# A streaming encoder layer on one core: the Vector engine's dependent instructions recorded apart

## The chip, the cores and the metric

The kernel runs on one core of a Trainium2 chip. The metric is the device time of one launch in microseconds (us); lower is better. Five engines work side by side, each with its own in-order queue: PE (matrix products; PEld is its weight load), DVE (vector work), ACT (activations and copies), POOL and SP (which here issues the transfers). They wait for one another, and an engine waits for its own earlier results, through semaphores.

## The reference

One layer of a hybrid trunk over 2048 prompt rows and 32 sample rows of width 1024. After a LayerNorm, one projection yields the inputs of two branches. Branch A is attention over a band of nine 64-row chunks. Branch B is a gated delta rule over 64-row chunks; cut to what matters here:

```python
m = einsum(k_beta, kb) * decay * strict
t_inv = triangular_solve(eye + m, eye)        # 64 x 64 for each chunk and head
u = t_inv @ v_beta
w = t_inv @ (k_beta * exp(gc))
def step(s, ...):                             # chunk after chunk
    v_new = u_c - w_c @ s
    o_c = (q_c * exp(gc_c)) @ s + qk_c @ v_new
    s = s * exp(g_last) + k_dec.T @ v_new
```

Both branches are gated, projected, merged and projected again, added to the scaled input, and normalised.

## The kernel before

The rows are done in two halves of 1024. For each half, phase B (the delta rule) is followed by phase A (attention); the merge of the branches and the last projection follow at the end. All the while 48 column tiles of the input weight, and a narrow 49th, are fetched, scaled, split into two 16-bit parts (`divide`, line 613) and multiplied with the normalised rows (`multiply`, line 657). These products write the tile `pj`. They are the filler of the PE queue throughout both phases.

**Phase B** works on blocks of eight chunks for a pair of heads, eight blocks a half, plus one block for the sample rows at the end of the second half: 17 blocks. For each block `system` (line 1160) makes the 64x64 systems, `solve` (line 1211) inverts their 32x32 diagonal parts with all 128 partitions at once by forward substitution, and `inverse` puts the 64x64 inverses together. Two `solve` streams run, so two blocks may be in substitution at once. `substitute` (line 1229) has 31 steps; each is a product `sys_t <- sys_u, sys_p` and a subtraction `sys_u <- sys_u, sys_t`, both on DVE, the second needing the first and the next product needing the second. That is 17 x 31 = 527 pairs.

`chain` (line 1305) then goes through the chunks in order. One step of it is a relay between PE and DVE: PE makes `x <- state, k_bd`, DVE makes `r`, PE makes `x <- r, u_bd`, DVE makes `vn`, PE makes `x <- vn, kd_bd`, DVE makes the new `state`. There are 132 steps. `tail` (line 1337) normalises a block's output; the lengths of its rows are worked out in the small tile `ms`.

**What sets the order.** Nothing here is scheduled by hand. Every piece of work is a Python generator, a stream, with a clock of its own. `Flow.run` (line 171) takes the stream with the lowest clock off a heap and lets it record instructions until its next `yield`. `Flow.spend` (line 191) charges each recorded instruction a modelled price and a hop (`HOP_SAME`, 0.12, where the stream's last instruction was on the same engine, `HOP` or `HOP_PE` otherwise) and moves the stream's clock. Instructions that stand between two yields therefore come out as neighbours, and each engine runs its instructions in exactly the recorded order. Where an instruction needs the result of an earlier one of its own engine, it carries a wait for it.

**Other names.** For each of the 49 weights `divide` computes a norm, a power of two `w_scale`, and from it the factors `w_inv` and `w_half`, which undo the scaling when the products leave PE. `h_scale` holds the same for the rows, made once by `norm_params`. In `system`, `inv`, `sc` and `gcb` (read there as `e_p`) lead from the squared lengths of k to the factors of the system's elements. `lengths` and `by_token` use the PSUM tile `b`, as do transposes.

Of the kernel before, what the change touches and what calls it, by code (L numbers as in the profile page):

```python
# [16 lines left out]
ALU = mybir.AluOpType  # L17
# [35 lines left out]
HOP_PE, HOP, HOP_SAME = 0.1, 0.2, 0.12  # L53
# [101 lines left out]
class Flow:  # L155
# [5 lines left out]
        self.heap, self.n, self.busy = [], 0, {}  # L161
        self.cur = Stream(None, 0.0)

    def push(self, s):
        self.n += 1
        heapq.heappush(self.heap, (s.clock, self.n, s))

    def start(self, gen, at=None):
        self.push(Stream(gen, self.cur.clock if at is None else at))
# [1 line left out]
    def run(self, until=None):  # L171
        outer = self.cur
        while self.heap and (until is None or until.at is None):
            s = heapq.heappop(self.heap)[2]
            self.cur = s
            try:
                what = next(s.gen)
            except StopIteration:
                continue
            if what is None:  # L180
                self.push(s)
            elif isinstance(what, float):
                s.clock = max(s.clock, what)
                self.push(s)
            else:
                what.ask(s)
        outer.clock = max(outer.clock, self.cur.clock)
        self.cur = outer
        assert until is None or until.at is not None, "a stream waits for good"
# [78 lines left out]
def trunk(ctx: ExitStack, tc: tile.TileContext, x_p, x_s, cache_k, cache_v, st_conv, st_gdn,  # L268
# [4 lines left out]
    flow = Flow()  # L273
# [98 lines left out]
    def norm_params(sp):  # L372

        prm0 = sp.tile([2 * KD, P], F32, name="prm0")
        dma(prm0[0:KD], ln0_g.rearrange("(k p) -> k p", p=P))
        yield dma(prm0[KD:2 * KD], ln0_b.rearrange("(k p) -> k p", p=P))
        yield bank["b"]
        ps = pt("b")
        PE.transpose(ps[:, 0:2 * KD], prm0[:], ident[0:2 * KD, 0:2 * KD])
        yield  # L380
        V.tensor_copy(ln0gT[:], ps[:, 0:KD])
        V.tensor_copy(ln0bT[:], ps[:, KD:2 * KD])
        bank["b"].give()

        top = sp.tile([P, 2, KD], F32, name="top")
        V.scalar_tensor_tensor(out=top[:, 0], in0=ln0gT[:], scalar=-1.0, in1=ln0gT[:], op0=ALU.mult, op1=ALU.max)
        V.scalar_tensor_tensor(out=top[:, 1], in0=ln0bT[:], scalar=-1.0, in1=ln0bT[:], op0=ALU.mult, op1=ALU.max)
        V.scalar_tensor_tensor(out=top[:, 0], in0=top[:, 0], scalar=D ** 0.5, in1=top[:, 1], op0=ALU.mult, op1=ALU.add)
        V.tensor_tensor(out=top[:, 1], in0=top[:, 0], in1=top[:, 0], op=ALU.mult)
        V.tensor_reduce(out=h_scale[:, 0:1], in_=top[:, 1], axis=AX.X, op=ALU.add)  # L390
        yield
        yield from power(h_scale[:, 1:2], h_scale[:, 0:1])
        V.reciprocal(out=h_scale[:, 2:3], in_=h_scale[:, 1:2])
        V.tensor_scalar(out=ln0gT[:], in0=ln0gT[:], scalar1=h_scale[:, 1:2], scalar2=None, op0=ALU.mult)
        V.tensor_scalar(out=ln0bT[:], in0=ln0bT[:], scalar1=h_scale[:, 1:2], scalar2=None, op0=ALU.mult)
        scaled.done()
# [186 lines left out]
    def fetch(jobs):  # L583
# [26 lines left out]
            yield raw_gate  # L610
        front_w.done()

    def divide():

        while True:
            job, raw, t = yield from q_raw.get()
            yield w_gate
            hi = wpool.tile([P, KD, P], F16, tag="whi", bufs=2, name="whi")
            lo = wpool.tile([P, KD, P], F16, tag="wlo", bufs=2, name="wlo")
            sc = w_scale[:, job.wid:job.wid + 1]  # L620
            yield t
            if job.half == 0:
                S.activation(out=hi[:], in_=raw[:], func=AF.Square, accum_out=w_sq[:])
                yield
                yield from power(sc, w_sq[:])
                inv = w_inv[:, job.wid:job.wid + 1]
                V.reciprocal(out=inv, in_=sc)
                V.tensor_scalar(out=inv, in0=inv, scalar1=h_scale[:, 2:3], scalar2=None, op0=ALU.mult)
                V.tensor_scalar(out=w_half[:, job.wid:job.wid + 1], in0=inv, scalar1=0.5, scalar2=None, op0=ALU.mult)
            src, main = raw[:, :, 0:job.cols], hi[:, :, 0:job.cols]  # L630
            S.activation(out=src, in_=src, func=AF.Copy, scale=sc)
            for i in range(2):
                ks = slice(4 * i, 4 * i + 4)
                S.copy(out=main[:, ks], in_=src[:, ks])
                yield

                rest_ = lo[:, ks] if job.cols == P else hi[:, ks, job.cols:P]
                G.tensor_tensor(out=rest_, in0=src[:, ks], in1=main[:, ks], op=ALU.subtract)
                if i:
                    raw_gate.give()  # L640
                    q_w.put((job, hi, lo))
                yield
# [133 lines left out]
    def phase_b(half):  # L776
# [383 lines left out]
        def system(k):  # L1160

            nch = k.nch
            n = nch * CH
            k.par = yield from par_slots.take()
            yield k.qk_ready
            yield k.prep
            k.pn = yield from p_slots.take()
            kb, qkb = k.kb, k.qkb = k_bd[k.par], qk_bd[k.par]
            p_c = k.p_c = p_cs[k.pn]
            qk, e_in, sc = k.qk, k.e_in, k.sc  # L1170
            s_p = sc[:, 1, 0:nch]
            for h in range(2):
                (S.copy if h else V.tensor_copy)(out=bdv(kb, h, nch), in_=chunked(hv(qk, h)[:, 1, 0:n]))
            ss = bp.tile([P, 2, 8], F32, tag="ss", bufs=9, name="ss")
            k.rr = bp.tile([P, 8], F32, tag="rr", bufs=9, name="rr")
            yield bank["b"]
            ps = pt("b")
            yield from lengths(k, 1, ss, ps, p_c)
            bank["b"].give()
            inv = bp.tile([P, 8], F32, tag="inv", bufs=2, name="inv")  # L1180
            V.reciprocal(out=inv[:, 0:nch], in_=ss[:, 1, 0:nch])
            V.scalar_tensor_tensor(out=s_p, in0=inv[:, 0:nch], scalar=0.25, in1=k.beta, op0=ALU.mult, op1=ALU.mult)
            e_p = k.gcb[:].rearrange("p (c i) -> p c i", i=HD)
            V.tensor_tensor(out=e_p[:, 0:nch], in0=e_in[:, 0:nch], in1=bcast(s_p, nch), op=ALU.mult)
            yield

            for g0 in range(0, nch, 4):
                g1 = min(nch, g0 + 4)
                yield bank["b"]
                ps = pt("b")  # L1190
                for c in range(g0, g1):
                    PE.matmul(ps[:, (c - g0) * P:(c - g0 + 1) * P], kb[:, c, :], qk[:, :, c * CH:(c + 1) * CH],
                              start=True, stop=True)
                    yield
                pv = ps[:, 0:(g1 - g0) * P].rearrange("p (c a d) -> p c a d", a=2, d=HD)
                V.tensor_tensor(out=p_c[:, g0:g1], in0=pv[:, :, 1, :], in1=e_p[:, g0:g1], op=ALU.mult)
                yield
                for h in range(2):
                    V.tensor_tensor(out=qkb[HS[h], g0:g1, HS[h]], in0=hv(pv, h)[:, :, 0, :],
                                    in1=hv(e_in, h)[:, g0:g1], op=ALU.mult)  # L1200
                bank["b"].give()
                yield

            dv = pd[k.n % (2 * NP)][:].rearrange("(c k) (j i) -> k j c i", k=4, i=32)
            for q in range(4):
                b = q % 2
                t = dma(dv[q][:, 0:nch], p_c[q * 32:q * 32 + 32, 0:nch, b * 32:b * 32 + 32])
            q_sys.put((k, t))
            flow.start(side(k, ss))
# [19 lines left out]
        def substitute(sys_p, sys_u, sys_t):  # L1229
            for j in range(31):  # L1230
                nr = j // 4 + 1
                w = 31 - j
                if nr == 1:
                    V.tensor_scalar(out=sys_t[:, 0, 0:w], in0=sys_p[:, j, j + 1:32], scalar1=sys_u[:, 0, j:j + 1],
                                    scalar2=None, op0=ALU.mult)
                else:
                    V.tensor_tensor(out=sys_t[:, 0:nr, 0:w], in0=sys_u[:, 0:nr, j:j + 1].to_broadcast([P, nr, w]),
                                    in1=sys_p[:, j:j + 1, j + 1:32].to_broadcast([P, nr, w]), op=ALU.mult)
                V.tensor_tensor(out=sys_u[:, 0:nr, j + 1:32], in0=sys_u[:, 0:nr, j + 1:32],
                                in1=sys_t[:, 0:nr, 0:w], op=ALU.subtract)  # L1240
                yield
# [95 lines left out]
        def tail(k):  # L1337
# [14 lines left out]
            m1 = ms[:, 1, 0:nch]  # L1352
            yield
            V.tensor_tensor(out=m0, in0=m0, in1=m1, op=ALU.mult)
            V.tensor_tensor(out=m0, in0=m0, in1=m1, op=ALU.mult)
            V.tensor_scalar(out=m0, in0=m0, scalar1=1.0 / HD, scalar2=NORM_EPS, op0=ALU.mult, op1=ALU.add)
            yield
            rsqrt(m2, m0)
# [936 lines left out]
```

## Time and profile before

| | |
|---|---|
| median of 3 runs | 2122.08 us (2121.66 to 2124.06) |
| the profiled execution | 2124.96 us |
| its span, first to last instruction | 2123.1 us |
| PE busy | 1994.4 us, 94% |
| DVE busy | 1534.2 us, 72% |
| ACT busy | 978.7 us, 46% |
| POOL busy | 634.3 us, 30% |
| mean granted PE clock | 0.98 |

The profile is of one execution. Nearly every instruction is recorded by the helper at line 259, so groups are told apart by the tiles that they write and read (written `out<-in`). In the trace the substitutions run from 142 to 479 us (first half) and from 955 to 1324 us (second half); the steps of the chain run from 210 to 522 us and from 1017 to 1342 us. Matmuls are pipelined and the ends that the profile gives them are modelled, so "PE busy" is not PE at its peak.

### The profile page before, as it was taken

The page shows a single profiled execution, that of the slowest core. Times are in us where ns is not written, and L with a number is a line of the kernel's source. Part 1 is how long each engine was busy: PE and PEld are TensorE (multiplying, and loading weights), DVE is VectorE, ACT ScalarE, POOL GpSimd, SP SyncE. Part 2 cuts the span into 40 slices and gives each one's busy share as a digit, 9 for nine tenths or more (in the row PEclk, how much of TensorE's full clock was granted, in tenths as well). Part 3 has the DMA queues.
Part 4 walks back from the last instruction along what each step waited for, and adds up shares of the span by engine and source line. Part 5 has one row for each costly group of instructions (what it writes and reads, how often), then busy time and mean ns, then how long its engine had stood idle before and what let it go on. Part 6 is the DMA issues. An engine that isn't in the chain of part 4 may idle for free. (4 is left out here: it accounts for less than half of the span.)

```text
span 2123.1 us, 41363 instructions
## 1 busy us (share of the span) xinstructions
PE 1994.4 (94%) x15098; PEld 1422.5 (67%) x15098; DVE 1534.2 (72%) x4660; ACT 978.7 (46%) x2098; POOL 634.3 (30%) x708
## 2 busy tenths in 40 slices
PE   4999898999999999999899999999999988999998
PEld 4454665666465656666666676767776777988896
DVE  7689989884277768779898987347657667766676
ACT  5655544443465667564444443346656652111110
POOL 6243333232322122333233232310110223443343
PEclk9999999899999999999999999999999999999999
DMA  3223232222423233222223233332322435443331
GB/s 120 75 84 102 76 88 78 67 79 82 122 67 120 82 93 99 70 73 76 58 70 94 62 86 85 99 100 72 92 77 67 138 120 191 128 123 103 116 107 61
DMA packets 197719, 196.49 MB, mean 93 GB/s; under 512 B 79622, under 2 KB 147570, under 8 KB 197516
## 3 DMA queue, kind: packets, MB, share of 16 engines
q1 hardware_dynamic: 197516, 193.85, 30.9%
q8 instruction: 119, 1.95, 0.4%
q14 instruction: 84, 0.69, 0.1%
HBM read 135.91 MB, written 50.53 MB: 88 GB/s over the span
## 5 line engine op out<-in xcount | busy, mean ns | idle before, releaser
L259 PE MATMUL pj<-hi,whi 128*128 128x512 f16 (+2 forms) x1992 | 650.7, 342 | 8.6 <-POOL whi L259 3.0
L259 PE MATMUL pj<-hi,wlo 128*128 128x512 f16 (+2 forms) x1952 | 640.8, 341 | 0.4 <-POOL wlo L259 0.4
L259 PEld LDWEIGHTS <-whi 128*128 128x128 f16 x3984 | 416.0, 106 | 217.5 <-issue 11.2
L259 PE MATMUL pj<-lo,whi 128*128 128x512 f16 (+2 forms) x1992 | 461.9, 340 | 0.0
L259 POOL TENSOR_TENSOR wlo<-wraw,whi 128x512 f16<-128x512 f32 x192 | 228.6, 1193 | 630.1 <-ACT whi L259 345.1
L259 PEld LDWEIGHTS <-wlo 128*128 128x128 f16 x1952 | 205.5, 105 | 108.5 <-issue 8.9
L259 ACT CAST mh<-sg 128x256 fp32r<-128x256 f32 x64 | 25.9, 407 | 276.1 <-DVE sg L259 276.0
L259 DVE TENSOR_TENSOR sys_u<-sys_u,sys_t 128x60 f32<-128x60 f32 (+24 forms) x527 | 135.7, 258 | 18.2
L259 PE MATMUL a<-ghi,whi 128*128 128x256 f32 (+1 forms) x512 | 134.8, 293 | 7.1 <-DVE sg L259 6.8
L259 ACT ACTIVATE wraw<-wraw,w_scale 128x1024 f32<-128x1024 f32 (+1 forms) x98 | 111.4, 1137 | 59.2 <-DVE w_scale L259 57.1
L259 ACT CAST ph<-b 128x512 f16<-128x512 f32 (+2 forms) x224 | 92.6, 422 | 92.7 <-PE b L259 86.1
L259 PE MATMUL a<-ghi,wlo 128*128 128x256 f32 (+1 forms) x512 | 131.9, 287 | 0.0
L259 ACT CAST whi<-wraw 128x512 f16<-128x512 f32 (+1 forms) x196 | 119.4, 611 | 27.1 <-PE pj L259 24.2
L259 DVE TENSOR_TENSOR pl<-b,ph 128x512 f16<-128x512 f32 (+2 forms) x224 | 107.6, 484 | 28.9 <-ACT ph L259 28.0
L259 DVE TENSOR_TENSOR sys_t<-sys_u,sys_p 128x54 f32<-128x54 f32 (+21 forms) x459 | 123.6, 269 | 4.0
L259 ACT ACTIVATE sb<-sb,mx,unit 128x640 f32<-128x640 f32 (+4 forms) x128 | 109.0, 852 | 25.5 <-DVE mx L259 25.1
L259 DVE SCALAR_TENSOR_TENSOR acc<-raw,cwT,acc 128x512 f32<-128x512 f32 x144 | 113.2, 786 | 8.4 <-ACT acc L259 7.4
L259 POOL TENSOR_TENSOR w_scale<-w_scale,mhalf 128x1 f32<-128x1 f32 x49 | 31.0, 633 | 288.0 <-DVE w_scale L259 230.1
L259 PEld LDWEIGHTS a<-ghi,whi 128*128 128x128 f32 x512 | 99.3, 194 | 8.8 <-DVE sg L259 7.9
L259 PE MATMUL b<-ident,sb 128*128 128x128 f32 x560 | 98.8, 276 | 2.9 <-ACT tmp L259 0.6
L259 ACT COPY v_t<-o 128x64 f32<-128x64 f32 x132 | 27.5, 209 | 158.3 <-PE o L259 121.5
L259 PEld LDWEIGHTS a<-ghi,wlo 128*128 128x128 f32 x512 | 98.9, 193 | 0.4 <-DVE wlo L259 0.2
(350 smaller groups left out, 4238.9 us busy)
## 6 DMA issues: line engine op xcount, KB each, us to landing
wraw<-in_w_in SPq DMA_DIRECT2D x192, 256.0 KB
sg<-sig SPq DMA_DIRECT2D x112, 128.0 KB
sig<-sig SPq DMA_DIRECT2D x44, 256.0 KB
sys_p<-sol_p SPq DMA_DIRECT2D x17, 512.0 KB
x<-in_x_p SPq DMA_DIRECT2D x16, 512.0 KB
xt<-in_x_p SPq DMA_DIRECT2D x16, 512.0 KB
out_y_p<-xt SPq DMA_DIRECT2D x16, 512.0 KB
glo<-g SPq DMA_DIRECT2D x14, 512.0 KB
```

What stands on the lines that cost most here:

```text
L259: r = f(*a, **k)
```

## The change

No computation is added but one small product (half of `h_scale`'s third column, made once). Some yields are added and one group of instructions is moved:

- in `substitute` a yield stands between product and subtraction;
- in `system` and `tail` yields stand between the dependent small instructions on `inv`, `sc`, `gcb` and on `ms`;
- the factors `w_inv` and `w_half` are made by a stream of their own, `factors`, so that the scaling of the weight on ACT no longer follows them in one stream. Both come straight from the reciprocal, with two ready factors, where before the second was made from the first;
- a stream whose last instruction was on DVE is put back on the heap `HOP_SAME` later (`push(s, later)`): streams are taken up by when DVE would be ready for them, not by when their last instruction ends.

```diff
@@ -161,9 +161,9 @@
         self.heap, self.n, self.busy = [], 0, {}
         self.cur = Stream(None, 0.0)
 
-    def push(self, s):
+    def push(self, s, later=0.0):
         self.n += 1
-        heapq.heappush(self.heap, (s.clock, self.n, s))
+        heapq.heappush(self.heap, (s.clock + later, self.n, s))
 
     def start(self, gen, at=None):
         self.push(Stream(gen, self.cur.clock if at is None else at))
@@ -178,7 +178,8 @@
             except StopIteration:
                 continue
             if what is None:
-                self.push(s)
+
+                self.push(s, HOP_SAME if s.last == "V" else 0.0)
             elif isinstance(what, float):
                 s.clock = max(s.clock, what)
                 self.push(s)
@@ -391,6 +392,7 @@
         yield
         yield from power(h_scale[:, 1:2], h_scale[:, 0:1])
         V.reciprocal(out=h_scale[:, 2:3], in_=h_scale[:, 1:2])
+        V.tensor_scalar(out=h_scale[:, 3:4], in0=h_scale[:, 2:3], scalar1=0.5, scalar2=None, op0=ALU.mult)
         V.tensor_scalar(out=ln0gT[:], in0=ln0gT[:], scalar1=h_scale[:, 1:2], scalar2=None, op0=ALU.mult)
         V.tensor_scalar(out=ln0bT[:], in0=ln0bT[:], scalar1=h_scale[:, 1:2], scalar2=None, op0=ALU.mult)
         scaled.done()
@@ -610,6 +612,14 @@
             yield raw_gate
         front_w.done()
 
+    def factors(wid):
+
+        inv, half_ = w_inv[:, wid:wid + 1], w_half[:, wid:wid + 1]
+        V.reciprocal(out=half_, in_=w_scale[:, wid:wid + 1])
+        yield
+        V.tensor_scalar(out=inv, in0=half_, scalar1=h_scale[:, 2:3], scalar2=None, op0=ALU.mult)
+        V.tensor_scalar(out=half_, in0=half_, scalar1=h_scale[:, 3:4], scalar2=None, op0=ALU.mult)
+
     def divide():
 
         while True:
@@ -623,10 +633,7 @@
                 S.activation(out=hi[:], in_=raw[:], func=AF.Square, accum_out=w_sq[:])
                 yield
                 yield from power(sc, w_sq[:])
-                inv = w_inv[:, job.wid:job.wid + 1]
-                V.reciprocal(out=inv, in_=sc)
-                V.tensor_scalar(out=inv, in0=inv, scalar1=h_scale[:, 2:3], scalar2=None, op0=ALU.mult)
-                V.tensor_scalar(out=w_half[:, job.wid:job.wid + 1], in0=inv, scalar1=0.5, scalar2=None, op0=ALU.mult)
+                flow.start(factors(job.wid))
             src, main = raw[:, :, 0:job.cols], hi[:, :, 0:job.cols]
             S.activation(out=src, in_=src, func=AF.Copy, scale=sc)
             for i in range(2):
@@ -1178,8 +1185,11 @@
             yield from lengths(k, 1, ss, ps, p_c)
             bank["b"].give()
             inv = bp.tile([P, 8], F32, tag="inv", bufs=2, name="inv")
+            yield
             V.reciprocal(out=inv[:, 0:nch], in_=ss[:, 1, 0:nch])
+            yield
             V.scalar_tensor_tensor(out=s_p, in0=inv[:, 0:nch], scalar=0.25, in1=k.beta, op0=ALU.mult, op1=ALU.mult)
+            yield
             e_p = k.gcb[:].rearrange("p (c i) -> p c i", i=HD)
             V.tensor_tensor(out=e_p[:, 0:nch], in0=e_in[:, 0:nch], in1=bcast(s_p, nch), op=ALU.mult)
             yield
@@ -1236,6 +1246,7 @@
                 else:
                     V.tensor_tensor(out=sys_t[:, 0:nr, 0:w], in0=sys_u[:, 0:nr, j:j + 1].to_broadcast([P, nr, w]),
                                     in1=sys_p[:, j:j + 1, j + 1:32].to_broadcast([P, nr, w]), op=ALU.mult)
+                yield
                 V.tensor_tensor(out=sys_u[:, 0:nr, j + 1:32], in0=sys_u[:, 0:nr, j + 1:32],
                                 in1=sys_t[:, 0:nr, 0:w], op=ALU.subtract)
                 yield
@@ -1352,7 +1363,9 @@
             m1 = ms[:, 1, 0:nch]
             yield
             V.tensor_tensor(out=m0, in0=m0, in1=m1, op=ALU.mult)
+            yield
             V.tensor_tensor(out=m0, in0=m0, in1=m1, op=ALU.mult)
+            yield
             V.tensor_scalar(out=m0, in0=m0, scalar1=1.0 / HD, scalar2=NORM_EPS, op0=ALU.mult, op1=ALU.add)
             yield
             rsqrt(m2, m0)
```

The list of instructions on PE, ACT, POOL and SP is the same as before in kind and number; DVE has 4663 for 4662. The order differs on every engine from the first transposes of the rows on; on DVE and POOL nearly to the end, while PE's last 2296 matmuls and weight loads and SP's last 192 transfers stand as before. Numbers behind names tell buffers apart.

**DVE, first half, where one substitution ends and the next begins** (`sys_t_3594` and `sys_t_4173` before, `sys_t_3595` and `sys_t_4187` in the change). Before:

```order
L259 TENSOR_TENSOR sys_t_3594<-sys_u_3593,sys_p_3592 128x8x2
L259 TENSOR_TENSOR sys_u_3593<-sys_u_3593,sys_t_3594 128x8x2
L259 SCALAR_TENSOR_TENSOR zb_4315<-zb_4315,pj_4239 128x512
L259 TENSOR_SCALAR vn_4345<-x_659,sc_2854 128x64
L259 TENSOR_TENSOR kd_bd0_623<-b_4321,swap_4304 64x4x64 x2
L259 TENSOR_SCALAR sys_t_4173<-sys_p_4171,sys_u_4172 128x30
L259 TENSOR_TENSOR sys_u_4172<-sys_u_4172,sys_t_4173 128x30
L259 TENSOR_TENSOR sys_t_3594<-sys_u_3593,sys_p_3592 128x8
L259 TENSOR_TENSOR sys_u_3593<-sys_u_3593,sys_t_3594 128x8
```

In the change:

```order
L260 TENSOR_SCALAR sys_t_4187<-sys_p_4185,sys_u_4186 128x31
L260 SCALAR_TENSOR_TENSOR r_4386<-x_634,negc_633,v_t1_630 128x64
L260 TENSOR_TENSOR sys_t_3595<-sys_u_3594,sys_p_3593 128x8x2
L260 TENSOR_TENSOR sys_u_4186<-sys_u_4186,sys_t_4187 128x31
L260 TENSOR_TENSOR sys_u_3594<-sys_u_3594,sys_t_3595 128x8x2
L260 TENSOR_SCALAR sys_t_4187<-sys_p_4185,sys_u_4186 128x30
L260 TENSOR_SCALAR vn_4397<-x_634,sc_2824 128x64
L260 TENSOR_TENSOR sys_t_3595<-sys_u_3594,sys_p_3593 128x8
L260 TENSOR_TENSOR sys_u_4186<-sys_u_4186,sys_t_4187 128x30
L260 TENSOR_TENSOR e_in_4410<-gcb_4317,col_632 128x512
L260 SCALAR_TENSOR_TENSOR state_118<-state_118,sc_2824,x_634 128x64
L260 TENSOR_TENSOR sys_u_3594<-sys_u_3594,sys_t_3595 128x8
```

Before, each subtraction stands directly behind its product. In the change there is a step of the other substitution, of the chain or of another block between the two. In the whole order the subtraction is its product's direct neighbour 527 times before and 151 times in the change; the next product is the subtraction's direct neighbour 78 and 147 times. All pairs of direct neighbours of which the second needs the first and waits for it fall from 1071 to 574.

**DVE, the factors of one weight**, a little later. Before:

```order
L259 TENSOR_SCALAR w_scale_128<-w_scale_128 128x1
L259 RECIPROCAL w_inv_129<-w_scale_128 128x1
L259 TENSOR_SCALAR w_inv_129<-w_inv_129,h_scale_126 128x1
L259 TENSOR_SCALAR w_half_130<-w_inv_129 128x1
L259 SCALAR_TENSOR_TENSOR state_118<-state_118,sc_2854,x_659 128x64
L259 TENSOR_TENSOR kd_bd0_623<-b_4321,sc_3870 64x4x64
L259 TENSOR_SCALAR sys_t_4173<-sys_p_4171,sys_u_4172 128x29
```

In the change:

```order
L260 TENSOR_TENSOR sys_t_4187<-sys_u_4186,sys_p_4185 128x2x25
L260 TENSOR_SCALAR w_scale_128<-w_scale_128 128x1
L260 TENSOR_TENSOR sys_u_4186<-sys_u_4186,sys_t_4187 128x2x25
L260 RECIPROCAL w_half_130<-w_scale_128 128x1
L260 TENSOR_SCALAR vn_4487<-x_634,sc_2824 128x64
L260 TENSOR_TENSOR sys_t_4187<-sys_u_4186,sys_p_4185 128x2x24
L260 COPY sc_4469<-ex_4471 128x8
L260 TENSOR_SCALAR w_inv_129<-w_half_130,h_scale_126 128x1
L260 TENSOR_SCALAR w_half_130<-w_half_130,h_scale_126 128x1
L260 SCALAR_TENSOR_TENSOR state_118<-state_118,sc_2824,x_634 128x64
```

The three instructions on the factors, a run in which each needed the one before, now stand apart, with steps of the chain and of the substitution between them.

**PE, one step of the chain in the same stretch**, from the product with `r` to the product with `vn`; `pj` are the projections that fill the queue. Before:

```order
L259 MATMUL x_659<-r_4393,u_bd1_631 128x64
L259 LDWEIGHTS whi_4080
L259 MATMUL pj_4411<-hi01_152,whi_4080 128x512
L259 MATMUL o_661<-state_118,q_bd1_619 128x64
L259 LDWEIGHTS wlo_4081
L259 MATMUL pj_4411<-hi01_152,wlo_4081 128x512
L259 LDWEIGHTS whi_4080
L259 MATMUL pj_4411<-hi01_152,whi_4080 128x512
L259 LDWEIGHTS wlo_4081
L259 MATMUL pj_4411<-hi01_152,wlo_4081 128x512
L259 MATMUL x_659<-vn_4416,kd_bd1_625 128x64
```

In the change:

```order
L260 MATMUL x_634<-r_4386,u_bd1_606 128x64
L260 LDWEIGHTS whi_3948
L260 MATMUL pj_4323<-lo01_153,whi_3948 128x512
L260 MATMUL o_636<-state_118,q_bd1_594 128x64
L260 MATMUL b_4403<-ident_106,v_t0_629 128x128 x4
L260 LDWEIGHTS whi_3948
L260 MATMUL pj_4323<-lo01_153,whi_3948 128x512
L260 MATMUL x_634<-vn_4397,kd_bd1_600 128x64
```

Four projections stood between the two; now two and a row of transposes do. Over all 132 steps the mean number of projections ahead of the product with `vn`, counted from the last product into `x`, falls from 4.04 to 3.45, and ahead of the product with `r` from 4.80 to 4.52.

## The prediction

> **What bounds the kernel now.** I read the page's first part first, then the busy time by stretches, then who waited for whom.
>
> ```profile
> span 2123.1 us, 41363 instructions
> PE 1994.4 (94%) x15098; PEld 1422.5 (67%) x15098; DVE 1534.2 (72%) x4660; ACT 978.7 (46%) x2098; POOL 634.3 (30%) x708
> core 0: us, PE busy (x) PEld busy (x) DVE busy (x) ACT busy (x) POOL busy (x), PEclk, DMA share, GB/s
> 142.00:210.00 68.00, 62.84 (x392) 34.07 (x391) 63.90 (x205) 37.19 (x66) 25.58 (x37) 0.97 0.33 90
> 210.00:479.00 269.00, 248.06 (x1851) 168.58 (x1849) 236.42 (x853) 122.96 (x260) 87.41 (x108) 0.96 0.29 80
> ...
> 955.00:1017.00 62.00, 56.25 (x442) 39.31 (x441) 58.62 (x184) 29.97 (x59) 20.42 (x34) 0.94 0.25 70
> 1017.00:1324.00 307.00, 281.60 (x2416) 208.84 (x2415) 263.66 (x950) 130.96 (x303) 91.72 (x122) 0.98 0.30 77
> ...
> 1790.00:2123.00 333.00, 322.85 (x2012) 290.94 (x2012) 228.36 (x366) 39.59 (x112) 127.97 (x100) 0.98 0.35 109
> ```
>
> Over the whole span PE is the bound: 94% busy, and its list of work does not change. So the time can change only by the time in which PE stands still. The two substitution regions (the four middle rows, 706 us together) are where it stands: it is idle there for 706 - 648.8 = 57 us by these rows, and DVE is busy for 622.6 us, 88%. The last row, 333 us, holds the merge, whose PE order the change leaves alone.
>
> Who ends PE's waits, and DVE's, while the chain runs (142 to 1342 us)?
>
> ```profile
> PE x L259 <- DVE vn L259: 15.4, 22, 1.3
> PE x L259 <- DVE r L259: 11.9, 19, 1.3
> PE x L259 <- DVE state L259: 8.1, 11, 2.3
> ...
> PE x L259 <- DVE sys_t L259: 5.1, 2, 2.7
> DVE state L259 <- PE x L259: 31.2, 54, 2.6
> ...
> DVE r L259 <- PE x L259: 22.3, 29, 5.5
> DVE vn L259 <- PE x L259: 14.6, 29, 1.1
> ```
>
> PE waits 15.4 + 11.9 + 8.1 + 5.1 = 40.5 us for DVE in the chain (the last of these is put down to a neighbour of the chain's instructions). DVE waits 31.2 + 22.3 + 14.6 = 68.1 us for PE. Neither bounds the chain alone. One step as the timeline shows it:
>
> ```profile
> 304.71 0.33 PE L259 MATMUL x<-state,k_bd 128*128 128x64 f32 x2
> ...
> 305.29 0.20 DVE L259 TENSOR_TENSOR sys_u<-sys_u,sys_t 128x42 f32<-128x42 f32 x1
> 305.41 0.14 DVE L259 TENSOR_SCALAR w_scale<-w_scale 128x1 int32<-128x1 int32 x1
> 305.59 0.16 DVE L259 RECIPROCAL w_inv<-w_scale 128x1 f32<-128x1 f32 x1
> ...
> 305.79 0.21 DVE L259 TENSOR_SCALAR w_inv<-w_inv,h_scale 128x1 f32<-128x1 f32 x1
> ...
> 306.04 0.15 DVE L259 TENSOR_SCALAR w_half<-w_inv 128x1 f32<-128x1 f32 x1
> ...
> 306.20 0.86 DVE L259 TENSOR_TENSOR kd_bd<-b,swap 64x256 f32<-64x256 f32 x2
> ...
> 307.07 0.20 DVE L259 TENSOR_TENSOR sys_t<-sys_u,sys_p 128x35 f32<-128x35 f32 x1
> 307.31 0.20 DVE L259 TENSOR_TENSOR sys_u<-sys_u,sys_t 128x35 f32<-128x35 f32 x1
> ...
> 307.54 0.28 DVE L259 SCALAR_TENSOR_TENSOR r<-x,negc,v_t 128x64 f32<-128x64 f32 x1
> ...
> 307.88 0.43 PE L259 MATMUL x<-r,u_bd 128*128 128x64 f32 x2 [0.67 <-DVE r L259]
> ```
>
> PE had finished `x` at 305.04; `r` started at 307.54. For 2.5 us it stood in DVE's queue behind weight factors and substitution, and PE then lost 0.67 us. This queue is what the change shortens.
>
> **What a dependent neighbour costs.** Each row's first number is its start.
>
> ```profile
> 316.25 0.21 DVE L259 TENSOR_TENSOR sys_t<-sys_u,sys_p 128x52 f32<-128x52 f32 x1
> 316.50 0.21 DVE L259 TENSOR_TENSOR sys_u<-sys_u,sys_t 128x52 f32<-128x52 f32 x1
> 316.63 0.28 DVE L259 SCALAR_TENSOR_TENSOR r<-x,negc,v_t 128x64 f32<-128x64 f32 x1
> 316.83 0.41 DVE L259 COPY k_bd<-qk 64x512 f32<-64x512 f32 x1
> L259 DVE TENSOR_TENSOR sys_u<-sys_u,sys_t 128x60 f32<-128x60 f32 (+24 forms) x527 | 135.7, 258 | 18.2
> L259 DVE TENSOR_TENSOR sys_t<-sys_u,sys_p 128x54 f32<-128x54 f32 (+21 forms) x459 | 123.6, 269 | 4.0
> ```
>
> The subtraction needs the product before it and starts 0.25 us after it. `r` does not need the subtraction and starts 0.13 us after it, before its recorded end. A dependent neighbour therefore costs 0.12 us of the queue more than an independent one, most of it inside the recorded duration and not seen as idle time (the 18.2 us of idle over 527 subtractions are only the rest).
>
> The Trainium skill ("VectorE: DVE Perf Modes", section "The DRAIN you can't avoid") says otherwise: the next Vector instruction does not start until the pipe is empty, and a semaphore between two costs nothing extra. The trace disagrees, since `r` started 0.08 us before the subtraction's recorded end; by that rule the whole sum below would be nothing and the time stays at 2122 us.
>
> **The change part by part.** Counts are of instructions in the recorded orders, prices from the rows above.
>
> - *Substitution.* 527 - 151 = 376 subtractions no longer stand right behind their product; 147 - 78 = 69 products more stand right behind their subtraction. Net 307 x 0.12 = 37 us of DVE, all in the two regions.
> - *Weight factors.* In the rows at 305.59, 305.79 and 306.04 the starts lie 0.20 and 0.25 us apart and the next 0.16; I take 0.1 us a pair. Dependent neighbours here fall from 147 to 35: 112 x 0.1 = 11 us, spread over the first half's 49 weights; about half, 6 us, fall into the first region. That ACT's scaling of the weight is recorded earlier is worth nothing: the row below has 3.0 us of PE waiting for a weight in the whole span. If this cover went, 3 us is also what is known of its cost.
> - *Scales and norms.* The neighbours on `inv`, `sc`, `gcb` fall from 51 to 0, those on `ms` from 29 to 5: 75 x 0.1 = 7 us.
> - *The small product in the start-up* stands ahead of the first transposes: at most the 0.21 us of a like instruction (305.79), once.
> - *The later take-up* adds no instruction. It changes places, on PE too. With the modelled gaps gone, the chain's products stand closer: 0.59 fewer projections before the product with `vn` and 0.28 fewer before the one with `r`. A projection takes 0.22 us (next rows), so PE reaches these two 0.13 and 0.06 us earlier. DVE must be that much earlier, or PE waits more.
>
> ```profile
> 305.75 0.38 PE L259 MATMUL pj<-hi,whi 128*128 128x512 f16 x1
> ...
> 305.97 0.38 PE L259 MATMUL pj<-hi,wlo 128*128 128x512 f16 x1
> L259 PE MATMUL pj<-hi,whi 128*128 128x512 f16 (+2 forms) x1992 | 650.7, 342 | 8.6 <-POOL whi L259 3.0 <-ACT hi L259 1.6 <-ACT sig L259 1.4
> ```
>
> DVE's work in the two regions so falls by 37 + 6 + 7 = 50 us of 706, 7%.
>
> *How much of it PE gets* no row shows, so bounds. At most it gets all 50 us: the 40.5 us of idle time are less than PE loses, since a projection's record lasts 0.38 us where the next starts after 0.22, so that up to 0.16 us of each wait hides behind a modelled end. At least it gets nothing, or loses: the closer places cost 132 x (0.13 + 0.06) = 25 us if DVE's results come no sooner. For the value I take the share of the mutual waits that lies on PE's side, 40.5 of 40.5 + 68.1, 0.37: where PE waits for DVE a shorter queue is time gained, where DVE waits for PE it is a longer wait. 50 x 0.37 = 19 us. What is late next there is PE's own product, `state <- x` with its 31.2 us.
>
> Against the profiled execution (2124.96 us, of which 1.9 lie outside the span) that is 2106 us. The execution stood 2.9 us above the median, so I forecast 2103 us.
>
> **Rivals.**
>
> 1. *DVE bounds these regions alone.* For it: DVE is 88% busy there, and most of the hops do not count as idle. Against it: it waits 68.1 us for PE in the chain. Then PE gets the whole 50 us: 2072 us.
> 2. *The freed time becomes idle time of DVE.* The chain's relay is then limited by PE's place in its own queue, and the saved hops lie between the steps and not in them. For it: the 31.2 us of `state <- x`. The result is 2118 to 2126 us. The skill's rule above gives the same by another way; against that one stand 0.13 and 0.25 us, and I leave it 0.03 of this rival's chance.
> 3. *Slower: PE comes too early.* The order now counts on DVE being ready. Two substitutions are open together for 419 of DVE's rows instead of 111, and one lasts 150 rows instead of 126, so a step of the chain meets other instructions as often as before, and each wide one among them (0.86 us for the pair at 306.20) hits a PE that has fewer projections left in front. This decides if `r` and `vn` come less than 0.06 and 0.13 us sooner after their PE product than now. The full 25 us would need DVE to gain nothing; half of it, 12 us, gives 2134 us.
> 4. *The change does not do what it says*: the pairs stay together. The order excludes it, 1071 neighbours against 574.
>
> **How the numbers follow.** Forecast, a partial gain of 5 to 28 us, 0.54; rival 1, a gain of more than 28 us, 0.18; rival 2, 0.14; rival 3, 0.14. About 0.2%, 4 us, is what a measurement of this kernel can tell from no change. Faster by more is the forecast and rival 1, 0.72; within it rival 2, 0.14; slower rival 3, 0.14. The range must leave out 0.2: it keeps the forecast, rival 2 and two thirds of rival 1 (down to 2080), and reaches up to 2126, where rival 3 begins. Reordering also shifts start-up and attention, where PE's waits are single ones; a few us either way are inside this.
>
> **What would show it.** In the changed profile the step from a product to its subtraction should hold other instructions, and DVE's busy time should fall by 35 to 60 us from 1534 us. PE's waits for `r`, `vn`, `state` should fall together from 40.5 us towards 20 us. The windows of phase B should hold the gain in both halves, and the stretch from the merge on should last 333 us as now. If DVE is less busy and these PE waits are as long, rival 2 holds; if they grow while DVE's waits for `x` shrink, rival 3. The forecast would be wrong from the start if a separated pair does not start its subtraction sooner, counted over both instructions.

## The result, and the profile after

The changed kernel takes 2086.23 us (median of 4 runs, 2083.65 to 2094.86) against 2121.87 us (4 runs, 2115.09 to 2124.06) for the kernel before: a ratio of 0.9844, with a 95% interval of 0.9809 to 0.9880. It is 1.6% faster. The forecast was 2103 us with a range of 2080 to 2126; the gain, 35.6 us, came out about twice the forecast's 19.

The page of the changed kernel (its profiled execution took 2083.65 us), its first part:

```profile
span 2081.6 us, 41386 instructions
PE 1968.6 (95%) x15098; PEld 1411.3 (68%) x15098; DVE 1499.7 (72%) x4661; ACT 978.1 (47%) x2098; POOL 633.1 (30%) x708
```

DVE is busy for 34.5 us less than the 1534.2 us of before, and the span is 41.5 us shorter. Busy time by stretches, the substitution regions (first four rows), one stretch for a later comparison, and the merge (each row: its start and end, its length, the busy time of the engines, PEclk, which is the clock granted to PE as a share of full speed, and the share and rate of the transfers):

```profile
core 0: us, PE busy (x) PEld busy (x) DVE busy (x) ACT busy (x) POOL busy (x), PEclk, DMA share, GB/s
143.00:213.00 70.00, 65.38 (x411) 35.27 (x409) 66.18 (x222) 39.31 (x71) 24.75 (x36) 1.00 0.35 95
213.00:467.00 254.00, 240.44 (x1849) 164.34 (x1850) 217.29 (x838) 124.50 (x259) 90.61 (x111) 0.98 0.31 84
937.00:1008.00 71.00, 63.52 (x503) 43.78 (x502) 65.86 (x203) 37.22 (x74) 23.36 (x38) 0.97 0.28 75
1008.00:1280.00 272.00, 258.58 (x2319) 197.05 (x2317) 242.15 (x926) 121.29 (x283) 87.48 (x117) 0.99 0.32 83
...
940.00:1345.00 405.00, 384.10 (x3298) 285.19 (x3296) 325.72 (x1189) 180.22 (x405) 129.76 (x170) 0.99 0.32 85
...
1749.00:2082.00 333.00, 320.77 (x2012) 288.11 (x2012) 224.03 (x365) 39.60 (x112) 126.00 (x100) 0.99 0.35 109
```

The regions shrank from 337 to 324 us and from 369 to 343 us: 39 of the 41.5 us are there, and the merge's 333 us are unchanged. PE stands still for 667 - 627.9 = 39 us of them (57 before); DVE is busy for 591.5 us, 89% (88% before). So the regions became shorter at the same load of DVE. Over the whole span PE's idle time fell by 15.7 us (2123.1 - 1994.4 = 128.7 before, 2081.6 - 1968.6 = 113.0 now), and the other 25.8 us came off its busy time, though its list of work is the same. Part of a wait hides behind the modelled ends, and the granted clock of these two executions differs, as a table below shows.

Who waits for whom from 142 to 1342 us (total, times, longest, in us):

```profile
PE x L260 <- DVE r L260: 14.5, 17, 2.3
PE x L260 <- DVE state L260: 4.8, 10, 0.9
...
PE x L260 <- DVE vn L260: 3.7, 8, 0.9
...
DVE state L260 <- PE x L260: 40.2, 72, 1.6
DVE vn L260 <- PE x L260: 17.6, 37, 1.6
DVE r L260 <- PE x L260: 14.0, 29, 1.3
```

PE's waits in the relay fell from 40.5 to 23.0 us: those for `vn` from 15.4 to 3.7 and those for `state` from 8.1 to 4.8, and the 5.1 us put down to `sys_t` are gone, while those for `r` rose from 11.9 to 14.5. DVE's rose a little, from 68.1 to 71.8 us, and moved to `state <- x` (40.2 us for 31.2), which the prediction named as what is late next. A separated pair in the timeline (start, duration), and the two groups of the substitution (busy time, mean ns, and behind the bar the idle time before them):

```profile
318.93 0.22 DVE L260 TENSOR_TENSOR sys_t<-sys_u,sys_p 128x66 f32<-128x66 f32 x1
319.06 0.42 DVE L260 TENSOR_TENSOR p_c<-b,gcb 128x256 f32<-128x256 f32 x1
...
320.00 0.22 DVE L260 TENSOR_TENSOR sys_u<-sys_u,sys_t 128x66 f32<-128x66 f32 x1
320.14 0.28 DVE L260 SCALAR_TENSOR_TENSOR r<-x,negc,v_t 128x64 f32<-128x64 f32 x1
```

```profile
L260 DVE TENSOR_TENSOR sys_u<-sys_u,sys_t 128x60 f32<-128x60 f32 (+23 forms) x527 | 129.3, 251 | 6.7
L260 DVE TENSOR_TENSOR sys_t<-sys_u,sys_p 128x60 f32<-128x60 f32 (+21 forms) x459 | 121.2, 265 | 6.1
```

Behind the product the next instruction starts after 0.13 us, where the dependent subtraction took 0.25. The idle time before the 527 subtractions fell from 18.2 to 6.7 us; before the 459 products it rose from 4.0 to 6.1.

### The profile page after: what moved, and what is told of

Its sections match the earlier page's. It is cut to its first block, busy times and chain, and to the rows that moved or that the text cites. A ratio compares the mean times of both kernels' runs of the same rounds, so it can differ in the third digit from the quotient of the medians.

```text
span 2081.6 us, 41386 instructions
## 1 busy us (share of the span) xinstructions
PE 1968.6 (95%) x15098; PEld 1411.3 (68%) x15098; DVE 1499.7 (72%) x4661; ACT 978.1 (47%) x2098; POOL 633.1 (30%) x708
## 5 line engine op out<-in xcount | busy, mean ns | idle before, releaser
L260 DVE TENSOR_TENSOR sys_u<-sys_u,sys_t 128x60 f32<-128x60 f32 (+23 forms) x527 | 129.3, 251 | 6.7
L260 DVE TENSOR_TENSOR sys_t<-sys_u,sys_p 128x60 f32<-128x60 f32 (+21 forms) x459 | 121.2, 265 | 6.1
```

The costliest lines, as they stand in the source:

```text
L260: r = f(*a, **k)
```

## The experiments

Three theories were open. **Queue**: the time saved between dependent neighbours shortens DVE's queue, and PE gets a part of it. **Order**: the later take-up, which adds and removes no instruction, changes where PE's products stand, for better or for worse. **Nothing new**: a dependent neighbour costs no more than an independent one, and the whole gain is an accident of the order. All ratios below are to the kernel before, measured beside it, with 95% intervals; where two are compared, 1% is 21 us.

### Is the gap between dependent neighbours free room?

An extra copy of 128x8, which nothing reads, stands between each product and its subtraction; it is not charged in the clocks, so that the order of all else stays that of before.

```diff
+                nc.vector.tensor_copy(junk[:], mhalf[:])
                 V.tensor_tensor(out=sys_u[:, 0:nr, j + 1:32], in0=sys_u[:, 0:nr, j + 1:32],
```

> The kernel before with one useless copy of 128x8 put between each product and its subtraction, not charged to the order's clocks: every other engine's order is that of before, DVE has 527 instructions more. A like copy in the trace of before takes 0.11 us of the queue. Theory Q (the wait between product and subtraction is free room): the copies fit into it, 2117 to 2130 us, and product to subtraction still takes some 0.25 us. Rival R (every DVE instruction waits for the one before it, dependent or not): 527 x 0.11 = 58 us more of DVE, and at the rate at which the change paid (36 us for 50) 2155 to 2170 us.

Ratio 1.0008 (0.9989 to 1.0026): 527 instructions more and no change. The timeline of this kernel and its groups:

```profile
316.86 0.21 DVE L259 TENSOR_TENSOR sys_t<-sys_u,sys_p 128x52 f32<-128x52 f32 x1
316.99 0.17 DVE L1240 COPY junk<-mhalf 128x8 f32<-128x8 f32 x1
317.11 0.21 DVE L259 TENSOR_TENSOR sys_u<-sys_u,sys_t 128x52 f32<-128x52 f32 x1
317.24 0.28 DVE L259 SCALAR_TENSOR_TENSOR r<-x,negc,v_t 128x64 f32<-128x64 f32 x1
```

```profile
L259 DVE TENSOR_TENSOR sys_u<-sys_u,sys_t 128x60 f32<-128x60 f32 (+24 forms) x527 | 122.8, 233 | 0.0
...
L1240 DVE COPY junk<-mhalf 128x8 f32<-128x8 f32 x527 | 102.1, 194 | 0.0
```

Product to subtraction is 0.25 us with the copy between them (0.13 + 0.12), as it was without. The 18.2 us of idle time before the subtractions are 0.0, and their mean duration fell from 258 to 233 ns. The copies show 102.1 us of busy time and cost nothing, which says how little the column "busy" tells of so small instructions. The theory that nothing is new, which expected 2155 to 2170 us here, falls with the 2122.63 us measured. The gap is room that an independent instruction as small as this copy has for nothing; a larger one was not tried.

### What is separating the pairs worth, with all else in its place?

The changed kernel, with each product charged in its old place and recorded directly before its subtraction. The orders of PE, ACT, POOL and SP are those of the changed kernel; on DVE there are 367 dependent neighbours more (941 for 574). The edit, cut to its new lines:

```diff
+                flow.spend("V", V.price("tensor_scalar" if nr == 1 else "tensor_tensor", (), k))
                 yield
+                what(**k)
                 V.tensor_tensor(out=sys_u[:, 0:nr, j + 1:32], in0=sys_u[:, 0:nr, j + 1:32],
```

> The changed kernel with each product recorded right in front of its subtraction, while the order's clocks are charged as if it stood in its old place: PE, ACT, POOL and SP have the changed kernel's order to the instruction, DVE has 527 products moved. Theory Q: DVE's queue loses what the separated pairs saved, 941 dependent neighbours for 574, 367 x 0.12 = 44 us of DVE; the time goes back to 2110 to 2125 us, or over the time before if PE's closer places now wait. Rival O: the time stays within 2082 to 2094 us, since every other engine's order is the one that brought the gain.

Ratio 0.9964 (0.9948 to 0.9979), 1.2% or 25 us above the changed kernel. Its page's row of the engines, and the group of the subtractions:

```profile
PE 1981.2 (94%) x15098; PEld 1415.1 (67%) x15098; DVE 1521.9 (72%) x4661; ACT 978.1 (46%) x2098; POOL 632.3 (30%) x708
```

```profile
L260 DVE TENSOR_TENSOR sys_u<-sys_u,sys_t 128x60 f32<-128x60 f32 (+23 forms) x527 | 131.8, 250 | 18.7 <-DVE sys_t L1253 0.5
```

The idle time before the subtractions is back, 18.7 us, and DVE is busy for 22.2 us more. PE's waits for `r`, `vn` and `state` are 16.6 + 11.3 + 4.3 = 32.2 us for 23.0. 367 x 0.12 = 44 us of DVE cost 25 us of time; by the two intervals the 25 are uncertain by about 8. No other engine's order differs, so DVE's queue alone made this difference, as the queue theory expected (2110 to 2125 us; 2112.66 measured). The edit also puts the products later among DVE's instructions; what that does beside the gap was not separated. What is left of the change without the separated pairs, the new order of the other engines among it, is 0.36%.

### The yields without the later take-up, and the later take-up without the yields

```diff
-                self.push(s, HOP_SAME if s.last == "V" else 0.0)
+                self.push(s)
```

> The changed kernel without the later take-up; all yields and the factors' own stream stay (636 dependent neighbours on DVE for 574). Theory Q: 62 pairs more, times 0.12 us is 7 us of DVE, at most 7 us back: 2086 to 2096 us. Rival O: most of the gain goes, 2105 to 2120 us.

Ratio 0.9922 (0.9897 to 0.9946).

The other half of it: the kernel before with nothing but the later take-up.

```diff
-                self.push(s)
+                self.push(s, HOP_SAME if s.last == "V" else 0.0)
```

> The kernel before with the later take-up alone; no yield is added, so the 527 subtractions stay right behind their products (1046 dependent neighbours on DVE for 1071 before). Theory Q (the shorter DVE queue makes the gain): nothing to speak of, 2116 to 2126 us. Rival O (the gain comes from the order on the other engines, which the later take-up moves): a good part of the 36 us is here already, 2095 to 2110 us.

Ratio 0.9893 (0.9859 to 0.9926). With both it is 0.9844. Both results, 2105.21 and 2100.23 us, lie where the order theory expected them and not the queue theory: dependent neighbours alone do not account for the gain. The yields alone are worth 0.78% and the later take-up alone 1.07%; on top of the yields the take-up adds 0.78% (0.9922 - 0.9844; about 0.4 points either way by the two intervals), about half of the whole gain; of the 2120 us of before that is 16.5 us. Yet it leaves the pairs as they were (1046 dependent neighbours for 1071). PE's waits for the relay, with the take-up alone, same stretch as above:

```profile
PE x L259 <- DVE vn L259: 12.9, 13, 1.8
PE x L259 <- DVE r L259: 10.5, 12, 1.8
PE x L259 <- DVE state L259: 6.2, 12, 1.1
```

29.6 us for 40.5, though DVE is as busy as before (1537.0 us). The recorded orders of PE show what differs: how many projections stand ahead of the relay's products, counted from the last product into `x`, the mean over 132 steps.

| kernel | ahead of the product with `r` | with `vn` |
|---|---|---|
| before | 4.80 | 4.04 |
| later take-up alone | 5.36 | 4.32 |
| yield in `substitute` alone | 3.53 | 2.83 |
| yield in `substitute` with take-up | 4.06 | 3.70 |
| yields alone | 4.04 | 3.02 |
| the change, take-up halved | 3.88 | 3.39 |
| the change (both) | 4.52 | 3.45 |
| the change, take-up doubled | 4.69 | 3.40 |

The yields pull the relay's products closer together; the full take-up pushes them apart, by 0.28 to 0.56 projections where it is added to before or to the yields. That it gains by giving DVE more time before PE asks for its result is a reading. For it: added to the yield in `substitute` alone, the take-up moves the two products furthest (0.53 and 0.87) and gains most, 1.17% (1.0034 - 0.9917, the latter below). Against it as the only reason: the halved take-up (ratio 0.9868, below) leaves `r` 0.16 projections closer than the yields alone (`vn` is 0.37 further) and gains all the same.

### Parts of the two

Three kernels more took single parts of the change. The yield in `substitute` alone (one line):

> The kernel before with the yield in the substitution alone: 199 subtractions right behind their product for 527, 206 products right behind their subtraction for 78, net 200 pairs x 0.12 = 24 us of DVE. Theory Q (DVE's queue, paid at 0.6 as the joined kernel showed): 14 us less, 2100 to 2110 us. Rival S (the small yields and the factors' own stream carry the yields' gain of some 15 us): 2113 to 2121 us.

Ratio 1.0034 (1.0020 to 1.0048): slower, though only 199 of the 527 subtractions still stand right behind their product. None of the theories expected that. Only the stream for the factors and the yields in `system` and `tail`:

> The kernel before with the yields in scales and norms and the factors' own stream, without the yield in the substitution and without the later take-up: 893 dependent neighbours for 1071. Theory Q: (115 + 71) x 0.1 = 19 us of DVE, of which some 13 in the substitution regions, at 0.6: 8 us less, 2108 to 2116 us. Rival L: outside of that; then the time at half clock in the profile says why, as with the substitution's yield alone (112 us at half clock for 84 before, which costs 14 us).

Ratio 1.0009 (0.9990 to 1.0029). The yield in `substitute` with the later take-up:

> The kernel before with the substitution's yield and the later take-up, without the small yields and the factors' own stream: 769 dependent neighbours. Theory Q and P together: the later take-up's 19 us and most of what the joined kernel lost, less the small ones' 8: 2088 to 2100 us. Rival L (the substitution's yield adds nothing, as it did alone): 2100 to 2110 us.

Ratio 0.9917 (0.9891 to 0.9943). The additions expected by the queue theory do not hold: apart, the two groups of yields cost 0.34% and nothing clear (0.09%, within its interval), and together they gain 0.78%, and with the take-up the yield in `substitute` adds nothing either (0.83% with it, 1.07% without, intervals overlapping). Only all of them together give the whole.

Then the take-up itself in two parts: only behind the chain's `r`, `vn` and `state`, or everywhere else. One of the three places, cut from the first edit:

```diff
                     V.scalar_tensor_tensor(out=r[:], in0=xs, scalar=k.negc[:, c:c + 1], in1=vc, op0=ALU.mult, op1=ALU.add)
-                    yield
+                    yield AFTER_V
```

> The kernel before with the later take-up for the chain's three DVE results alone (r, vn, state), whose next instruction is PE's. Theory P (the later take-up, 19 us alone, pays because PE's product with a DVE result is recorded behind one projection more and so does not stand in PE's queue waiting for it): most of it is here, 2098 to 2108 us. Rival T (it pays elsewhere, in the order on DVE or in the other streams): 2114 to 2124 us. Rival L (luck: any shift of the order moves the time by 10 to 20 us either way): anything from 2100 to 2135 us, and not the sum with the complement below.

Ratio 0.9952 (0.9936 to 0.9967).

> The complement: the kernel before with the later take-up for every stream but at those three places of the chain. Theory P: little, 2112 to 2122 us. Rival T: most of the 19 us, 2098 to 2108 us. Rival L: as there; this gain and that of the chain alone do not add up to 19 us.

Ratio 0.9995 (0.9977 to 1.0013). The chain's three places give 0.48%, the others nothing, and both together 1.07%. In the first of the two the product with `r` stands behind 4.97 projections and that with `vn` behind 4.48, in the second behind 4.16 and 4.03 (4.80 and 4.04 before). The gain stands with the larger numbers, though the second loses 0.64 projections ahead of `r` and is no slower. And PE's waits in the relay are not shorter in the first (18.5 + 15.5 + 3.9 + 2.4 = 40.3 us by its trace), so its gain does not pass through them, and where it comes from was not found.

### Why the yield in `substitute` alone is slower

PE's waits in that kernel from 940 to 1345 us, the longest (the relay's own, from 142 to 1342 us, are down to 10.9 + 3.3 + 3.2 + 0.5 + 2.2 = 20 us):

```profile
PE pj L259 <- DVE z_s L259: 6.2, 1, 6.2
PE pj L259 <- DVE zb L259: 5.3, 3, 3.1
...
PE b L259 <- ACT z_c L259: 3.4, 2, 2.7
PE b L259 <- DVE tu_t L259: 3.0, 1, 3.0
```

These are single waits of other streams. From 950 to 1360 us PE waits for DVE in the relay 9.0 us, 21.6 before, but in all its other waits 23.4 us, 8.7 before. What follows the first of them, in the timeline and in stretches of 3.4 us (PEclk is the last column but two; the first row is the whole region):

```profile
1110.18 0.41 PE L259 MATMUL pj<-hi,whi 128*128 128x272 f16 x1 [6.25 <-DVE z_s L259]
```

```profile
core 0: us, PE busy (x) PEld busy (x) DVE busy (x) ACT busy (x) POOL busy (x), PEclk, DMA share, GB/s
940.00:1345.00 405.00, 371.77 (x3029) 274.10 (x3028) 332.11 (x1159) 170.84 (x381) 122.35 (x162) 0.93 0.28 77
...
1102.60:1106.00 3.40, 1.33 (x7) 0.39 (x4) 3.16 (x14) 1.12 (x3) 1.15 (x1) 0.99 0.26 72
1106.00:1109.40 3.40, 0.00 (x0) 0.00 (x0) 3.09 (x12) 0.00 (x0) 1.17 (x2) 0.50 0.57 173
1109.40:1112.80 3.40, 2.62 (x12) 1.79 (x13) 2.85 (x15) 2.86 (x5) 0.17 (x1) 0.50 0.21 39
1112.80:1116.30 3.50, 3.50 (x18) 2.32 (x16) 3.15 (x14) 0.00 (x0) 0.00 (x0) 0.51 0.72 195
```

The granted clock is 0.50 until 6 us after the wait has ended. Over the 405 us of the first row it is 0.93; in the same stretch of the kernel before it is 0.97, and PE gets through 3141 matmuls instead of 3029; in the changed kernel it is 0.99, with 3298 (shown above). Every execution has its clock listed with its span, so the time lost at half clock, (1 - clock) x span, can be set beside the time (it counts half clock while PE stands still too):

| kernel (executions) | median span | median clock | lost at half clock |
|---|---|---|---|
| before (21) | 2118.4 | 0.983 | 36.0 |
| yield in `substitute` alone (10) | 2126.8 | 0.977 | 48.9 |
| pairs joined again (10) | 2110.7 | 0.983 | 35.9 |
| yields alone (7) | 2103.2 | 0.983 | 35.8 |
| later take-up alone (4) | 2098.5 | 0.981 | 39.9 |
| small yields and factors alone (10) | 2120.4 | 0.9855 | 30.7 |
| the change (4) | 2084.3 | 0.9875 | 26.1 |
| the change, take-up doubled (4) | 2082.1 | 0.983 | 35.4 |

Among the 89 executions of the changed and altered kernels, each taken about its own kernel's mean, 1 us lost at half clock goes with 0.74 us of span (correlation 0.82). So the yield in `substitute` alone lost 12.9 us more than before and is 8.4 us longer. By this account the single waits and the clock behind them ate what the queue gave; no run takes them away, so it is argued and not shown. The change lost 9.9 us less than before, by the slope an estimate of 7 to 10 of its 34 us. (The profiled execution of before, at 0.980, makes that share look larger: 42.5 for 25.0 us.) But the clock does not order the kernels: with the take-up doubled the time is as short at the clock of before, and the small yields alone lost 5.3 us less than before without being faster.

### Is the size of the take-up right?

The changed kernel with 0.24, with 0.06, and with 0.12 also for streams whose last instruction was on ACT or POOL (here each line for itself):

```diff
-                self.push(s, HOP_SAME if s.last == "V" else 0.0)
+                self.push(s, 2 * HOP_SAME if s.last == "V" else 0.0)
+                self.push(s, 0.5 * HOP_SAME if s.last == "V" else 0.0)
+                self.push(s, HOP_SAME if s.last in ("V", "S", "G") else 0.0)
```

> The changed kernel with the later take-up twice as large, 0.24. Theory P: PE's products move behind another projection, and with 480 dependent neighbours for 574 DVE's queue is shorter still; PE's waits fall but each step of the chain lasts longer; 2078 to 2092 us, the same within some us. Rival L: 2095 us or more is as likely as that.

Ratio 0.9842 (0.9810 to 0.9875).

> The changed kernel with the later take-up half as large, 0.06. Without it 2105 us, with 0.12 us 2086, with 0.24 us 2084. Theory P (a mechanism with a size): in between, 2088 to 2100 us. Rival L (each order has its own luck): outside of that as likely as inside.

Ratio 0.9868 (0.9826 to 0.9911).

> The changed kernel with the later take-up also for streams whose last instruction was on ACT or POOL; 562 dependent neighbours for 574. If it pays that what comes from another engine stands one projection further back in PE's queue, the ACT results gain too: 2076 to 2086 us. If DVE's results were the only late ones, PE is served later for nothing: 2086 to 2096 us.

Ratio 0.9866 (0.9825 to 0.9907). With 0, 0.06, 0.12 and 0.24 the ratios are 0.9922, 0.9868, 0.9844 and 0.9842. Any of the three sizes is better than none, the half one only just beyond the intervals; beyond 0.12 nothing is gained, and no version beats the change by more than the intervals.

## Why the prediction was right, and what it got wrong

The direction and the place were right, and so was the mechanism that was priced, the dependent neighbours in DVE's queue. A second gain of about the same size was priced at nothing or less, and the time is 17 us below the forecast. The gain of 35.6 us lies outside the forecast's own part of the range (5 to 28 us), in the part that was kept for rival 1, though rival 1's reason did not hold. That the range held the result is in part luck.

- **A dependent neighbour costs 0.12 us more.** Shown at the places looked at: filled with a copy the gap costs nothing, and joined again, 367 pairs cost 25 us. The Trainium skill ("VectorE: DVE Perf Modes", section "The DRAIN you can't avoid"), read as the prediction read it, would have given no gain; these runs decide against that reading. The section itself adds that a next instruction which is not held starts earlier, and so leaves room for the 0.13 us.
- **DVE's saving, 50 us.** Its busy time fell by 34.5 us, 0.5 us short of the 35 to 60 foretold. Part of the saving was never busy time: 11.5 us came off the idle time before the subtractions.
- **PE's share, 0.37.** The forecast's 19 us for the yields stand against 0.78%, 16.5 us, measured without the take-up. That they agree is partly luck: the sum adds up parts, and apart these parts gain nothing. In the sharper test 25 of 44 us, 0.57, reached the time; without the 7 to 10 us that the clock differs there (35.9 for 26.1 us lost), an estimate, it is 0.34 to 0.41. These are two ways of counting and not one measurement.
- **The later take-up: the step that failed.** It was priced at nothing, or at up to -25 us, because the whole change has fewer projections ahead of the relay's products, and that was put down to it. The variants split this: the yields do that (4.80 to 4.04, 4.04 to 3.02), and the take-up does the opposite (back to 4.52 and 3.45). It is worth 0.78% on top of the yields and 1.07% alone, of which the chain's own three places have 0.48%. By the prediction's own price of a projection, 132 x (0.48 + 0.43) x 0.22 = 26 us of room in PE's queue; 16.5 us were measured. That the room makes the gain is not shown.
- **Time at half clock was not in the sum.** The prediction said that the time can change only by the time in which PE stands still. In the profiles 25.8 of the 41.5 us came off PE's busy time, and 17.5 us less were lost at half clock (42.5 for 25.0). Over all executions the clock's part is nearer 7 to 10 us, an estimate, and the doubled take-up is as fast without it.
- **Rivals.** "DVE bounds alone" expected the whole 50 us in the time, 2072 us; against it as a cause stand the 71.8 us that DVE still waits in the relay. "Idle time of DVE" falls with the 2086 us. "PE comes too early" is refuted for the change as a whole, whose relay waits fell, though those for `r` did not. The one slower kernel, the yield in `substitute` alone, does have the relay's products closest, but its relay waits less; what grew there are other streams' waits.

**What stays open.** The parts do not add up: apart, the two groups of yields lose 0.43% together, and jointly they gain 0.78%. A new order thus seems to bring something like half a per cent of its own, an estimate from these sums; which wait happens to be long and where the clock drops may be how. Of the take-up's gain the room in PE's queue is a reading of the recorded orders and of the shorter waits with it alone; a kernel that moves only PE's products was not tried. That it gains at three sizes, and without the yields, speaks for a mechanism and against luck, but how much of the 16.5 us is which isn't settled.

## What to carry to other kernels

In an engine that runs many small instructions in order, as DVE does here, the pair to look for is a result used by the very next one: its cost hides in the durations, and two start times in the timeline (0.25 and 0.13 us here) show it better than any busy or idle column. Put independent work between them, but let what decides the order know the same gap, here that half was worth as much as the first. That it pays because PE is not sent for the result too early is likely, not shown. Judge single parts of such a change only with the clock and their own intervals beside them, since a new order alone seems to move the time by about half a per cent here.

## What the hardware showed beside this

Half clock can follow short waits. The kernel before, timeline and stretches after one wait of 2.68 us:

```profile
1156.58 0.41 PE L259 MATMUL x<-r,u_bd 128*128 128x64 f32 x2 [2.68 <-DVE sys_t L259]
```

```profile
core 0: us, PE busy (x) PEld busy (x) DVE busy (x) ACT busy (x) POOL busy (x), PEclk, DMA share, GB/s
1154.80:1158.30 3.50, 1.72 (x15) 1.54 (x16) 2.38 (x7) 0.65 (x2) 1.07 (x1) 1.00 0.06 9
1158.30:1161.70 3.40, 3.40 (x20) 2.87 (x18) 2.72 (x8) 0.03 (x1) 0.00 (x0) 0.50 0.45 76
1161.70:1165.10 3.40, 3.40 (x33) 2.98 (x32) 3.32 (x7) 1.75 (x3) 0.42 (x1) 0.99 0.75 205
```

PE is fully busy again when its clock falls to 0.50 for one stretch, in which it makes 20 matmuls where the next makes 33. The drop comes after the wait, so the profile books it as busy time and not as idle: behind a wait of 2.7 us about 1.7 us of PE's work were lost (half of the 3.4 us), an estimate. It does not always follow: in the clock records of all 14 traces, half clock sets in during 17 of the 34 idle gaps of PE of 2.5 to 3.0 us or within 4 us of their end. That such a wait causes the drop was not tested. The Trainium skill ("TensorE: Matmul & The Clock Gate", section "HAM oscillation — how this bites in real kernels") gives the rule as no PE-idle gaps of more than about 3.4 us; here a drop stands behind a shorter one.
